# A hybrid scan and attention block on one core: keys handled in three tasks, context decay and rotation tied behind weight chunks, result stores on ScalarE's queue

## The chip, the cores and the metric

The kernel runs on one core of a Trainium2 chip. The metric is device time in microseconds (us), the median of several executions. The engines of the core are named as the profile names them: PE is TensorE (matmuls), DVE is VectorE, ACT is ScalarE, POOL is GpSimd, SP is SyncE. SP, ACT and POOL each have a queue from which they issue DMA transfers, and each engine works through its instructions in the order in which they stand.

## The reference

One transformer block over 256 tokens and 256 context tokens, width 2048. Both are normalised and modulated, then multiplied by one wide matrix `w_in`, whose columns are cut into the inputs of two branches:

```python
xn = rmsnorm(h, norm_gain[l]) * (1.0 + scale) + shift
cn = rmsnorm(hc, norm_gain[l]) * (1.0 + scale_c) + shift_c
aq, ak, av, ag, hq, hff, hfb, hi, hg, ma, mb = split_columns(xn @ w_in[l])
...
q = apply_axial_rope(aq...) * q_scale
k = apply_axial_rope(ak...)
att_branch = window_attention(q, k, v, k_c, v_c, sink_logits[l]) * silu(ag)
```

The other branch, HGRN2, is a two-way gated scan with 16 heads of 128: the forget gates `hff` and `hfb` give a decay per key, the context's own decay gives the state from which the scan starts (forward and backward), and the scan's output is normalised and gated by `silu(hg)`. At the end

```python
y = sigmoid(m_a + b_m[0]) * (hg_branch @ w_o_hgrn) + sigmoid(m_b + b_m[1]) * (att_branch @ w_o_attn)
out = rmsnorm(h + gate * (y @ w_out), final_norm_gain)   # the residual add and the final norm
```

## The kernel before

Everything hangs on weights that stream through once. A weight **chunk** (`wchunk`) is a 512 KB piece of a matrix: SP's queue loads it into a tile `raw` (5 buffers), ACT copies it into `wh` (the leading bits, L78), DVE subtracts to get `wl` (the rest, L79), three buffers each. PE then multiplies: in `proj_tok_g` a chunk is eight matmuls with `wh` (lines L93 and L94 in turn) and four with `wl` (L96). The low ones come last, so `wl` may be late by the time of the eight.

PE runs the instructions in the order in which the code is written (`tc.manual_schedule` names PE alone). On DVE, ACT, POOL and SP a scheduler sets the order by priorities; `wchunk` stands under a high priority, so that the next `wh` and `wl` come first whenever their inputs are due. `tc.issue_after(i)` holds what is written under it back in that order until instruction `i` has been placed: it sets an order and adds no wait of its own.

The program has a start (norms, modulation), a stage that makes forgets, values and keys and stores them in DRAM scratch, eight **pairs** (n = 0 to 7, some 72 us each, 652 to 1270 us in the trace), then attention and the output projections. A pair does the scan of two heads (`pair`), woven with filler (`weave`, `with_gates`, `inputs`) that keeps PE fed: `side_work` is a chain of projection **blocks** (`output_gate`, `merge_out`, `attn_queries`, `attn_gates`), each eight chunks or so. What goes with the blocks and is touched here:

- `output_gate(g)` makes the tiles `sgg`, `attn_queries(j)` the rotated queries `qr`, `attn_gates(j)` the tiles `sga`; each is stored to DRAM scratch (`hg`, `qr`, `ag`) and read back later. `merge_out` stores its tiles `sgm` (`ma`, `mb`) from ACT's queue (L1059).
- `attn_keys(z, t)`: four tasks, one for each half z (0: the 256 tokens, whose keys are rotated; 1: the context's) and row tile t. A task fetches `kr` from scratch `kv`, rotates it into `kx` where z is 0 (`rope`: products with the cosines L1064, with the sines L1069, sum L1072), and is later turned on PE (`turn_tile`, L1092: four transposes into `tkt`), then split by ACT and DVE (L1094, L1095). `inputs` calls `tasks_on` at steps 7, 10, 13 and 16 of the 20 steps of a pair: it finishes the task that was begun at the step before and begins the next.
- `load_forgets(n + 1)`: in the course of pair n it loads the two forget tiles of the next pair (`F0`, `F1`, L1151) and then calls `ctx_decay` for each, which takes a running product over the context half. That is on POOL a memset of `e` (L773 forward, L777 backward), on DVE two scans (L774 or L778) and one combining step (L779).
- `gates` fills in a long product on DVE (L197) whose rows `hgw` are loaded by POOL (L526).

The tiles `sgg`, `sga`, `sgm`, `qr`, `kr`, `kx`, `vr`, `e` and `hsum` all come from one set of **three buffers** (tag "sm"). Whoever takes one waits until the one that held it is done, and if that was a store, until the store has landed.

Of the kernel before, what the change touches and what calls it, by code (L numbers as in the profile page):

```python
# [7 lines left out]
F32 = mybir.dt.float32  # L8
F32R = mybir.dt.float32r
U8 = mybir.dt.uint8  # L10
AF = mybir.ActivationFunctionType
# [27 lines left out]
def block_kernel(ctx: ExitStack, tc: tile.TileContext, x, c, cx, c_ctx, w_ada, b_ada, norm_gain, w_in,  # L39
# [26 lines left out]
            nc.sync.dma_start(rv[:, g], w[row0: row0 + nk * P, co: co + ncol].rearrange("(k p) c -> p k c", p=P))  # L66
        return raw, rv

    last_lo = [None]

    def wchunk(w, row0, nk, col0, ncol):
        cl = col0 if isinstance(col0, tuple) else (col0,)
        raw, rv = wload(w, row0, nk, cl, ncol)
        h = wp.tile([P, 1024], F32R, tag="wh", name="wh", bufs=3)
        lo = wp.tile([P, 1024], F32R, tag="wl", name="wl", bufs=3)
        n = len(cl) * nk * ncol
        with tc.high_priority(PRIO):
            act.activation(h[:, :n], raw[:, :n], AF.Copy)  # L78
            last_lo[0] = dve.tensor_tensor(lo[:, :n], raw[:, :n], h[:, :n].bitcast(F32), op=ALU.subtract).ins  # L79
        parts = [(h[:, g * nk * ncol: (g + 1) * nk * ncol].rearrange("p (k c) -> p k c", k=nk),  # L80
                  lo[:, g * nk * ncol: (g + 1) * nk * ncol].rearrange("p (k c) -> p k c", k=nk)) for g in range(len(cl))]
        return parts if isinstance(col0, tuple) else parts[0]
# [428 lines left out]
    def run(g):  # L511
        for _ in g:
            pass

    def output_gate(g):
        bg = yield from proj_tok_g(w_in, C_HG + 512 * g, x_st, range(2))
        for t in range(2):
            sg = base.tile([P, 512], F32, tag="sm", name="sgg", bufs=3)
            act.activation(sg, bg[t], AF.Sigmoid)
            dve.tensor_tensor(sg, bg[t], sg, op=ALU.mult)  # L520
            nc.gpsimd.dma_start(hg_dr[g][:, t * 512: (t + 1) * 512], sg)

    def gates():

# [21 lines left out]
    with pl("sp", reuse_waits="tile") as sp:  # L546
# [182 lines left out]
        with tc.manual_schedule(engines={mybir.EngineType.PE}):  # L729
            bv0 = proj_tok(w_in, C_HI, x_st, range(4))  # L730
            for g in range(2):
                token_sums(g)
            for t in range(2):
                vo = fp.tile([P, 2, 512], F32, tag="F0", name="vo", bufs=2)
                with tc.high_priority(2 * PRIO):
                    act.activation(vo[:, 0, :], bv0[t], AF.Copy)
                    dve.tensor_copy(vo[:, 1, :], bv0[2 + t])
                nc.gpsimd.dma_start(v_dr[0][t], vo.rearrange("p a c -> p (a c)"))
            run(output_gate(0))
            for g in range(1, 4):  # L740
# [320 lines left out]
    def rope(dst, src, t):  # L1061

        cos = cs[:, K_COS + t * HD: K_COS + (t + 1) * HD].unsqueeze(1).unsqueeze(1).to_broadcast([P, 2, 2, HD])
        dve.tensor_tensor(dst, src.rearrange("p (r h d) -> p r h d", r=2, h=2), cos, op=ALU.mult)  # L1064
# [7 lines left out]
        dve.tensor_tensor(dst, dst, tf, op=ALU.add)  # L1072
# [7 lines left out]
    tasks, task = [], [None]  # L1080

    def tasks_on():


        if task[0]:
            task[0]()
        task[0] = tasks.pop(0)() if tasks else None

    def turn_tile(src, dst, scale=1.0):
        tk = ps.tile([P, 512], F32, tag="tp", name="tkt")  # L1090
        for j in range(4):
            pe.transpose(tk[:, j * P: (j + 1) * P], src[:, j * HD: (j + 1) * HD], ident)  # L1092
        tk = tk.rearrange("p (r c) -> p r c", r=dst[0].shape[1])
        act.activation(dst[0], tk, AF.Copy, scale=scale)  # L1094
        dve.scalar_tensor_tensor(dst[1], tk, scale, dst[0].bitcast(F32), op0=ALU.mult, op1=ALU.subtract)  # L1095

    def attn_keys(z, t):
        def fetch():
            kr = base.tile([P, 512], F32, tag="sm", name="kr", bufs=3)
            nc.gpsimd.dma_start(kr, kv_dr[0][t][:, z * 512: (z + 1) * 512])  # L1100
            if z == 0:
                kx, kr = kr, base.tile([P, 512], F32, tag="sm", name="kx", bufs=3)
                rope(kr.rearrange("p (r h d) -> p r h d", r=2, h=2), kx, t)
            return lambda: turn_tile(kr, [X[:, z: 8: 2, t * P: (t + 1) * P] for X in (XH, XL)])
        return fetch

    def attn_values():
        for t in range(4):
            vr = base.tile([P, 512], F32, tag="sm", name="vr", bufs=3)
            nc.gpsimd.dma_start(vr, kv_dr[1][t % 2][:, (t // 2) * 512: (t // 2 + 1) * 512])  # L1110
            rows = slice(8 + 2 * t, 10 + 2 * t)
            split(XH[:, rows, :], XL[:, rows, :], vr.rearrange("p (r c) -> p r c", r=2))
            yield

    def attn_queries(j):

        def fetch(t):
            qr = base.tile([P, 512], F32, tag="sm", name="qr", bufs=3)
            nc.gpsimd.dma_start(qr, qr_dr[j][:, t * 512: (t + 1) * 512])

            def then():
                q = [XL[:, 8 + 4 * z + 2 * t: 10 + 4 * z + 2 * t, :] for z in range(2)]
                turn_tile(qr, q, HD ** -0.5)
                for z in range(2):
                    nc.gpsimd.dma_start(q_dr[j][z][:, t * 512: (t + 1) * 512].rearrange("p (r c) -> p r c", r=2),
                                        q[z].bitcast(F32))
            return then

        bq = yield from proj_tok_g(w_in, C_Q + 512 * j, x_st, range(2))
        for t in range(2):  # L1130
            qr = base.tile([P, 512], F32, tag="sm", name="qr", bufs=3)
            rope(qr.rearrange("p (r h d) -> p r h d", r=2, h=2), bq[t], t)
            nc.gpsimd.dma_start(qr_dr[j][:, t * 512: (t + 1) * 512], qr)
            tasks.append(lambda t=t: fetch(t))

    def attn_gates(j):
        for hf in range(2):
            bg = yield from proj_col_x_g(w_in, C_G + 512 * j + 256 * hf)
            for i, b in enumerate(bg):
                gs = halves_sum(b, "bb", 2)  # L1140
                sg = base.tile([P, 512], F32, tag="sm", name="sga", bufs=3)[:, :T]
                act.activation(sg, gs, AF.Sigmoid)
                dve.tensor_tensor(sg, sg, gs, op=ALU.mult)
                c0 = (2 * hf + i) * T
                nc.gpsimd.dma_start(ag_dr[j][:, c0: c0 + T], sg)

    def load_forgets(n):
        F = [None, None]
        for d in range(2):
            F[d] = fp.tile([P, 2, 512], F32, tag=f"F{d}", name=f"F{d}", bufs=2 - d)  # L1150
            nc.gpsimd.dma_start(F[d].rearrange("p i t -> p (i t)"), F_dr[d][n])  # L1151
            yield
        for d in range(2):
            ctx_decay(F, (d,))
            yield
        return F

    def side_work():
        values = attn_values()
        tasks.extend(attn_keys(z, t) for z in range(2) for t in range(2))  # L1160
        blocks = (output_gate(1), merge_out(0, 0), output_gate(2), attn_queries(0), merge_out(0, 1), output_gate(3),
                  attn_queries(1), merge_out(0, 2), attn_gates(0), merge_out(0, 3), attn_queries(2), merge_out(1, 0),
                  attn_gates(1), merge_out(1, 1), attn_queries(3), merge_out(1, 2), attn_gates(2), merge_out(1, 3),
                  attn_gates(3))
        for n, g in enumerate(blocks):
            for k, got in enumerate(g):
                yield got
                if n > 16 and k % 2:
                    next(values, None)
            yield 0  # L1170

    side = side_work()
    SIDE = (20, 20, 20, 20, 20, 20, 20, 31)
# [361 lines left out]
```

## Time and profile before

| what | us |
|---|---|
| median of three runs (lowest, highest) | 1605.37 (1603.41, 1609.92) |
| the profiled execution's own time | 1600.81 |
| its span, first to last instruction | 1599.0 |
| PE busy in the span | 1570.7 (98%) |
| DVE busy | 1182.7 (74%) |
| ACT busy | 855.4 (53%) |
| POOL busy | 157.6 (10%) |
| mean granted clock of TensorE | 0.996 |

In the lines of the profile, `wl<-raw,wh` means that the instruction writes tile wl from raw and wh, and L79 is line 79 of the kernel. A timeline row gives the start, the duration, the engine (ACTq is the DMA issuing part of ACT), the instruction, how many are joined in the row (x4), and in square brackets how long the engine stood idle before it and what ended that. A row's duration for matmuls overlaps with the next row's: their pace is the distance of the starts.

### The profile page before, as it was taken

How to read it: one execution, taken by the hardware profiler on the slowest of the kernel's cores; microseconds unless marked ns; L12 is line 12 of the kernel's file. 1: busy time of each engine (PE TensorE's matmuls, PEld its weight loads, DVE VectorE, ACT ScalarE, POOL GpSimd, SP SyncE). 2: the span in 40 equal slices, each digit the busy share in tenths (PEclk: the TensorE clock that was granted, in tenths of full speed). 3: DMA queues.
4: the chain of work that ended last, by engine and by line, in shares of the span. 5: the costliest groups of instructions: out<-in, count | busy, mean ns of one | idle time of the engine just before them, and what ended most of it. 6: DMA issues, size and time to landing. Idle time of an engine off the chain costs nothing.

```text
span 1599.0 us, 27552 instructions
## 1 busy us (share of the span) xinstructions
PE 1570.7 (98%) x10810; PEld 1343.6 (84%) x10810; DVE 1182.7 (74%) x1745; ACT 855.4 (53%) x1338; POOL 157.6 (10%) x312
## 2 busy tenths in 40 slices
PE   7999999999999999999999999999999999999998
PEld 4567899999888888878888888788888888888887
DVE  4449677777888888786978887887977677757764
ACT  4334343333555555656566566565566776744442
POOL 2000000000000000111122222122112100000000
PEclk9999999999999999999999999999999999999999
DMA  9995533434444444776778787676788754558761
GB/s 368 386 386 175 160 120 127 138 130 129 148 134 132 132 132 132 250 235 219 234 251 282 248 266 240 223 263 218 249 275 277 254 160 157 158 172 281 231 209 69
DMA packets 238290, 333.81 MB, mean 209 GB/s; under 512 B 12080, under 2 KB 155856, under 8 KB 237392
## 3 DMA queue, kind: packets, MB, share of 16 engines
q1 hardware_dynamic: 212048, 249.54, 47.8%
q0 software_dynamic: 21216, 70.38, 12.8%
q10 hardware_dynamic: 4896, 12.13, 2.2%
q8 instruction: 85, 1.39, 0.4%
q14 instruction: 45, 0.37, 0.1%
HBM read 300.53 MB, written 31.47 MB: 208 GB/s over the span
## 4 chain that ended last, share of the span: by engine, by line
PE 90%; DMA 4%; DVE 3%; issue 2%; ACT 1%; SPq 0%; POOL 0%; POOLq 0%; DVEq 0%; ACTq 0%
PE pj L93 13%; PE pj L96 13%; PE pj L94 13%; PE pj L147 7%; PE pm L645 4%; PE pj L150 4%; PE pj L645 3%; PE pj L717 2%; PE pj L722 2%; PE pj L719 2%; PE pm L648 2%; PE pm L717 2%; PE pm L722 2%; PE pm L719 2%; PE pj L648 2%
## 5 line engine op out<-in xcount | busy, mean ns | idle before, releaser
L78 ACT ACTIVATE wh<-raw 128x1024 fp32r<-128x1024 f32 x292 | 307.2, 1059 | 262.3 <-PE pj L94 175.2
L79 DVE TENSOR_TENSOR wl<-raw,wh 128x1024 fp32r<-128x1024 f32 x292 | 354.8, 1222 | 125.3 <-ACT wh L78 121.5
L93 PE MATMUL pj<-wh,xHL 128*128 128x512 f32 (+1 forms) x832 | 326.2, 393 | 0.7 <-ACT sg L212 0.7
L94 PE MATMUL pj<-wh,xHL 128*128 128x512 f32 (+1 forms) x832 | 321.4, 388 | 0.0
L96 PE MATMUL pj<-wl,xHL 128*128 128x512 f32 (+1 forms) x832 | 219.7, 388 | 3.6 <-DVE wl L79 3.6
L93 PEld LDWEIGHTS pj<-wh,xHL 128*128 128x128 f32 x832 | 157.4, 189 | 33.1 <-ACT sg L212 1.9
L96 PEld LDWEIGHTS pj<-wl,xHL 128*128 128x128 f32 x832 | 154.6, 189 | 35.5 <-DVE wl L79 4.0
L94 PEld LDWEIGHTS pj<-wh,xHL 128*128 128x128 f32 x832 | 157.6, 189 | 30.2
L620 ACT ACTIVATE wh<-T 128x1024 fp32r<-128x1024 f32 x69 | 73.2, 1061 | 150.9 <-DVE T L601 75.5
L620 ACT ACTIVATE wh<-raw 128x1024 fp32r<-128x1024 f32 x92 | 96.8, 1054 | 62.2 <-PE pj L719 20.2
L147 PE MATMUL pj<-xHL,wh 128*128 128x512 f32 x512 | 129.9, 395 | 0.0
L621 DVE TENSOR_TENSOR wl<-raw,wh 128x1024 fp32r<-128x1024 f32 x92 | 112.1, 1219 | 7.4 <-ACT wh L620 7.3
L147 PEld LDWEIGHTS pj<-xHL,wh 128*128 128x128 f32 x512 | 92.5, 189 | 16.8
L621 DVE TENSOR_TENSOR wl<-T,wh 128x1024 fp32r<-128x1024 f32 x69 | 84.2, 1221 | 28.8 <-ACT wh L620 28.8
L150 PEld LDWEIGHTS pj<-xHL,wl 128*128 128x128 f32 x512 | 69.9, 190 | 5.5 <-issue 0.5
L150 PE MATMUL pj<-xHL,wl 128*128 128x256 f32 x512 | 71.6, 283 | 0.3 <-issue 0.3
L197 DVE SCALAR_TENSOR_TENSOR acc<-hgw,cg,acc 128x512 f32<-128x512 f32 x60 | 44.9, 749 | 29.6 <-DMA hgw<-in_w_ada_dram 29.5
L902 DVE TENSOR_TENSOR A<-A,X 128x512 f32<-128x512 f32 x96 | 61.9, 687 | 1.5 <-ACT Kmt L832 0.7
L526 POOL DMA_DIRECT2D hgw<-in_w_ada_dram x64 | 34.8, 544 | 263.8 <-DVE acc L197 210.0
L645 PE MATMUL pm<-S,wh 128*128 128x512 f32 x224 | 56.7, 395 | 0.8 <-ACT s L652 0.7
L601 DVE TENSOR_TENSOR T<-raw,T 128x1024 f32<-128x1024 f32 x46 | 56.1, 1219 | 0.0
L601 DVE TENSOR_TENSOR raw<-raw 128x1024 f32<-128x1024 f32 x23 | 28.2, 1225 | 35.3 <-DMA raw<-in_w_in_dram 35.3
(359 smaller groups left out, 3037.9 us busy)
## 6 DMA issues: line engine op xcount, KB each, us to landing
raw<-in_w_in_dram SPq DMA_DIRECT2D x300, 512.0 KB, 4.5
raw<-in_w_ada_dram SPq DMA_DIRECT2D x64, 512.0 KB, 8.0
hgw<-in_w_ada_dram POOLq DMA_DIRECT2D x64, 256.0 KB, 4.4
raw<-in_w_o_hgrn_dram SPq DMA_DIRECT2D x32, 512.0 KB, 3.6
raw<-in_w_o_attn_dram SPq DMA_DIRECT2D x32, 512.0 KB, 4.3
raw<-in_w_out_dram SPq DMA_DIRECT2D x28, 512.0 KB, 3.9
F<-F POOLq DMA_DIRECT2D x16, 512.0 KB, 6.6
F<-F ACTq DMA_DIRECT2D x13, 512.0 KB, 4.4
```

What stands on the lines that cost most here:

```text
L78: act.activation(h[:, :n], raw[:, :n], AF.Copy)
L79: last_lo[0] = dve.tensor_tensor(lo[:, :n], raw[:, :n], h[:, :n].bitcast(F32), op=ALU.subtract).ins
L93: pe.matmul(o, s[0], m[0], start=first, stop=False)
L94: pe.matmul(o, s[1], m[0], start=False, stop=False)
L96: pe.matmul(o, s[0], m[1], start=False, stop=last)
L147: pe.matmul(o.rearrange("p (a t) -> p a t", a=2), h[:, j, cs_], xHL[:, :, k0 + j, :T], start=k0 + j == 0, stop=False)
L150: pe.matmul(o[:, :T], lo[:, j, cs_], xH[:, k0 + j, :T], start=False, stop=k0 + j == KT - 1)
L601: dve.tensor_tensor(o, x_, y_, op=ALU.subtract)
L620: act.activation(h, src, AF.Copy)
L621: dve.tensor_tensor(lo, src, h.bitcast(F32), op=ALU.subtract)
L645: pe.matmul(m_[z].rearrange("p (z a t) -> p z a t", z=2, a=2), h[:, k, :], mv(k), start=fresh and k == 0, stop=False, skip_group_check=True)
L648: pe.matmul(pairs_of(m_[z][:, :T]), lo[:, k, :], mv(k)[:, 0], start=False, stop=k == 7, skip_group_check=True)
```

## The change

Four parts. (1) The task of a rotated key is cut in three: fetch at one slot, rotate at the next, turn at the third; the rotation is written under `behind_chunk()`, and it reads `kr` and writes `kx` (before, the loaded tile was named `kx` and the rotated one `kr`). (2) `behind_chunk()` places what stands in it after the latest `wh` on ACT and the latest `wl` on DVE. It is put around the rotation of the keys, around `ctx_decay` (once a chunk has been written), around the split of the attention values, and around the sending of stores. (3) The stores of `sgg`, `qr` and `sga` are no longer issued on POOL's queue where the tile is made; they are put on a list (`outs`) and issued on ACT's queue by `send()` at the next block's first chunk (for `sga` also within the block). A query's fetch task is appended only when its store is sent. (4) Each of the four steps of `attn_values` becomes two, fetch and split, and they are run at each step of the last blocks instead of every second.

```diff
-    last_lo = [None]
+    last_hi, last_lo = [None], [None]
+    def behind_chunk():
+        both = ExitStack()
+        both.enter_context(tc.issue_after(last_hi[0]))
+        both.enter_context(tc.issue_after(last_lo[0]))
+        return both
...
+    outs, tasks, task = [], [], [None]
+    def send():
+        while outs:
+            o = outs.pop(0)
+            nc.scalar.dma_start(*o[:2])
+            tasks.extend(o[2:])
...                                     # output_gate
-            nc.gpsimd.dma_start(hg_dr[g][:, t * 512: (t + 1) * 512], sg)
+            outs.append((hg_dr[g][:, t * 512: (t + 1) * 512], sg))
...
             run(output_gate(0))
+            send()
...                                     # tasks_on
-        if task[0]:
-            task[0]()
-        task[0] = tasks.pop(0)() if tasks else None
+        task[0] = (task[0]() if task[0] else None) or (tasks.pop(0)() if tasks else None)
...                                     # attn_keys: fetch
-            if z == 0:
-                kx, kr = kr, base.tile([P, 512], F32, tag="sm", name="kx", bufs=3)
-                rope(kr.rearrange("p (r h d) -> p r h d", r=2, h=2), kx, t)
-            return lambda: turn_tile(kr, [X[:, z: 8: 2, t * P: (t + 1) * P] for X in (XH, XL)])
+            dst = [X[:, z: 8: 2, t * P: (t + 1) * P] for X in (XH, XL)]
+            if z:
+                return lambda: turn_tile(kr, dst)
+            def rotate():
+                kx = base.tile([P, 512], F32, tag="sm", name="kx", bufs=3)
+                with behind_chunk():
+                    rope(kx.rearrange("p (r h d) -> p r h d", r=2, h=2), kr, t)
+                return lambda: turn_tile(kx, dst)
+            return rotate
...                                     # attn_values
+            yield
             rows = slice(8 + 2 * t, 10 + 2 * t)
-            split(XH[:, rows, :], XL[:, rows, :], vr.rearrange("p (r c) -> p r c", r=2))
+            with behind_chunk():
+                split(XH[:, rows, :], XL[:, rows, :], vr.rearrange("p (r c) -> p r c", r=2))
...                                     # attn_queries
-            nc.gpsimd.dma_start(qr_dr[j][:, t * 512: (t + 1) * 512], qr)
-            tasks.append(lambda t=t: fetch(t))
+            outs.append((qr_dr[j][:, t * 512: (t + 1) * 512], qr, lambda t=t: fetch(t)))
...                                     # attn_gates
-            bg = yield from proj_col_x_g(w_in, C_G + 512 * j + 256 * hf)
+            cols_ = proj_col_x_g(w_in, C_G + 512 * j + 256 * hf)
+            for k in range(4):
+                yield next(cols_)
+                if k == 0 and outs:
+                    with behind_chunk():
+                        send()
+            bg = result(cols_)
...
-                nc.gpsimd.dma_start(ag_dr[j][:, c0: c0 + T], sg)
+                outs.append((ag_dr[j][:, c0: c0 + T], sg))
...                                     # load_forgets
-            ctx_decay(F, (d,))
+            with behind_chunk() if last_lo[0] else ExitStack():
+                ctx_decay(F, (d,))
...                                     # side_work
-                if n > 16 and k % 2:
+                if outs and k == 0:
+                    with behind_chunk():
+                        send()
+                if n > NB - 3:          # NB = 19
                     next(values, None)
             yield 0
+        send()
```

How this moves instructions is seen in the order in which each engine has them. Names carry numbers here: `kx_6698` is one tile. Lines after the change are shifted (`wl` is L86 instead of L79, the matmuls L100, L101 and L103 instead of L93, L94 and L96, the turn L1104 instead of L1092).

**PE in pair 0, where a key is turned.** Before, between the low matmuls of one chunk and the high ones of the next:

```order
L96 MATMUL pj_6575<-wl_6747,xHL_84 128x512
L96 MATMUL pj_6576<-wl_6747,xHL_84 128x512
L1092 MATMUL tkt_6762<-cs_78,kx_6698 128x128 x4
L93 MATMUL pj_6575<-wh_6773,xHL_84 128x512
L94 MATMUL pj_6575<-wh_6773,xHL_84 128x512
```

After, the same place:

```order
L103 MATMUL pj_6567<-wl_6732,xHL_84 128x512
L103 MATMUL pj_6568<-wl_6732,xHL_84 128x512
L1104 MATMUL tkt_6747<-cs_78,kx_6681 128x128 x4
L100 MATMUL pj_6567<-wh_6758,xHL_84 128x512
L101 MATMUL pj_6567<-wh_6758,xHL_84 128x512
```

Before, this is the turn of the second key (t = 1), fetched one slot earlier; after, it is the turn of the first key (t = 0), fetched two slots earlier. The second key's turn now stands in pair 1.

**DVE at the same place** (the rows between two `wl`). Before: `kx_6698` is the second key's loaded and rotated tile, `A` and `X2` belong to the scan of pair 0, `acc` to the long product.

```order
L902 TENSOR_TENSOR A_6346<-A_6346,X2_6347 128x64x8 x2
L79 TENSOR_TENSOR wl_6774<-raw_6771,wh_6773 128x1024
L197 SCALAR_TENSOR_TENSOR acc_6232<-hgw_6234,cg_87,acc_6232 128x512
L1064 TENSOR_TENSOR kx_6698<-kr_6696,cs_78 128x512
L1069 TENSOR_TENSOR rt_6700<-kr_6696,cs_78 128x8x32 x2
L902 TENSOR_TENSOR A_6346<-A_6346,X2_6347 128x32x16 x2
L79 TENSOR_TENSOR wl_6800<-raw_6797,wh_6799 128x1024
L1072 TENSOR_TENSOR kx_6698<-kx_6698,rt_6700 128x512
```

After (`kx_6681` is the first key's rotated tile, `kr_6537` its loaded one; its products with the sines stand three chunks earlier):

```order
L535 TENSOR_TENSOR sgg_6559<-pj_6380,sgg_6559 128x512
L535 TENSOR_TENSOR sgg_6562<-pj_6381,sgg_6562 128x512
L86 TENSOR_TENSOR wl_6732<-raw_6729,wh_6731 128x1024
L918 TENSOR_TENSOR A_6346<-A_6346,X2_6347 128x128x4 x2
L1080 TENSOR_TENSOR kx_6681<-kr_6537,cs_78 128x512
L887 COPY_PREDICATED X2_6347<-mk_79,al_6587 128x4x32
L1088 TENSOR_TENSOR kx_6681<-kx_6681,rt_6683 128x512
L887 COPY_PREDICATED X2_6347<-mk_79,al_6587 128x4x32
L918 TENSOR_TENSOR A_6346<-A_6346,X2_6347 128x64x8 x2
L887 COPY_PREDICATED X2_6347<-mk_79,al_6587 128x4x32
L86 TENSOR_TENSOR wl_6759<-raw_6756,wh_6758 128x1024
```

The rotation that shares a place with this turn now belongs to a key fetched two slots earlier, and its first product with the cosines stands ahead of `wl_6759`; it writes a buffer that `sgg_6559` held.

**POOL's and ACT's queues at the same place.** Before, POOL stores the two `sgg` and fetches the key behind them:

```order
L521 DMA hg1_116<-sgg_6565 128x512
L521 DMA hg1_116<-sgg_6569 128x512
L1151 DMA F1_6722<-F1_1_100 128x1024
L1100 DMA kr_6696<-kv0_1_128 128x512
L1100 DMA kr_6769<-kv0_0_127 128x512
L526 DMA hgw_6234<-in_w_ada_dram 128x512
L773 MEMSET e_6789 128x1 x2
```

After, ACT issues them behind the next chunk's `wh`:

```order
L534 ACTIVATE sgg_6559<-pj_6380 128x512
L534 ACTIVATE sgg_6562<-pj_6381 128x512
L85 ACTIVATE wh_6731<-raw_6729 128x1024
L527 DMA hg1_116<-sgg_6559 128x512
L527 DMA hg1_116<-sgg_6562 128x512
L884 ACTIVATE X2_6347<-al_6587 128x4x32
```

The stores have gone from POOL's queue to ACT's, one chunk later; the second key's fetch is now `kr_6754` on POOL, and its rotation stands two chunks further on.

**DVE in pair 4, the context decay of pair 5.** `e_10017` is the backward scan's tile, `F1_9895` the forget tile that it reads. Before:

```order
L79 TENSOR_TENSOR wl_9920<-raw_9917,wh_9919 128x1024
L197 SCALAR_TENSOR_TENSOR acc_6232<-hgw_6234,cg_87,acc_6232 128x512
L902 TENSOR_TENSOR A_9518<-A_9518,X2_9519 128x128x4 x2
L871 COPY_PREDICATED X2_9519<-mk_79,al_9783 128x4x32 x2
L778 SCALAR_TENSOR_TENSOR e_10017<-F1_9895,zero_6228 128x255
L871 COPY_PREDICATED X2_9519<-mk_79,al_9783 128x4x32
L778 SCALAR_TENSOR_TENSOR e_10017<-F1_9895,zero_6228 128x255
L902 TENSOR_TENSOR A_9518<-A_9518,X2_9519 128x64x8 x2
L779 SCALAR_TENSOR_TENSOR F1_9895<-F1_9895,e_10017 128x2x256
L79 TENSOR_TENSOR wl_9940<-raw_9937,wh_9939 128x1024
```

After:

```order
L86 TENSOR_TENSOR wl_9940<-raw_9937,wh_9939 128x1024
L790 SCALAR_TENSOR_TENSOR e_9955<-F0_9671,zero_6228 128x255 x2
L918 TENSOR_TENSOR A_9518<-A_9518,X2_9519 128x32x16 x2
L795 SCALAR_TENSOR_TENSOR F0_9671<-F0_9671,e_9955 128x2x256
L86 TENSOR_TENSOR wl_9964<-raw_9961,wh_9963 128x1024
L918 TENSOR_TENSOR A_9518<-A_9518,X2_9519 128x16x32 x2
L86 TENSOR_TENSOR wl_9982<-raw_9979,wh_9981 128x1024
L204 SCALAR_TENSOR_TENSOR acc_6232<-hgw_6234,cg_87,acc_6232 128x512
L86 TENSOR_TENSOR wl_10002<-raw_9999,wh_10001 128x1024
L794 SCALAR_TENSOR_TENSOR e_10017<-F1_9895,zero_6228 128x255 x2
```

The scan that reads `F1_9895` stood between `wl_9920` and `wl_9940`; now it stands behind `wl_10002`, four chunks later, and the four `wl` between are ahead of it. POOL's memset of `e_10017` and its load of `F1_9895` stay in the same order to each other.

More of the change, by code (lines that the diff above doesn't have):

```diff
@@ L77, in wchunk @@
         with tc.high_priority(PRIO):
-            act.activation(h[:, :n], raw[:, :n], AF.Copy)
+            last_hi[0] = act.activation(h[:, :n], raw[:, :n], AF.Copy).ins
             last_lo[0] = dve.tensor_tensor(lo[:, :n], raw[:, :n], h[:, :n].bitcast(F32), op=ALU.subtract).ins
@@ L1078, in split @@
         dve.tensor_tensor(dl, src, dh.bitcast(F32), op=ALU.subtract)
-    tasks, task = [], [None]
     def tasks_on():
-        if task[0]:
-            task[0]()
-        task[0] = tasks.pop(0)() if tasks else None
+        task[0] = (task[0]() if task[0] else None) or (tasks.pop(0)() if tasks else None)
     def turn_tile(src, dst, scale=1.0):
@@ L1158, in side_work @@
     def side_work():
-        values = attn_values()
+        values, NB = attn_values(), 19
         tasks.extend(attn_keys(z, t) for z in range(2) for t in range(2))
```

## The prediction

> **What bounds the kernel now.** I read the page's head and chain first, to see which engine sets the time; then what PE waited for in the eight pairs, since the change lies there; then the timelines of the two places that this list names, engine by engine, back to the transfer at their root.
>
> From the page:
>
> ```profile
> span 1599.0 us, 27552 instructions
> PE 1570.7 (98%) x10810; PEld 1343.6 (84%) x10810; DVE 1182.7 (74%) x1745; ACT 855.4 (53%) x1338; POOL 157.6 (10%) x312
> ...
> PE 90%; DMA 4%; DVE 3%; issue 2%; ACT 1%; SPq 0%; POOL 0%; POOLq 0%; DVEq 0%; ACTq 0%
> ```
>
> PE is the bound. The change adds and removes no matmul, so it can win only where PE stands still or runs slowly. PE's waits between 652 and 1270 us (total, times, longest):
>
> ```profile
> PE tkt L1092 <- DVE kx L1072: 3.9, 1, 3.9
> PE pj L96 <- DVE wl L79: 3.6, 1, 3.6
> PE al L977 <- ACT X L868: 0.4, 1, 0.4
> PE pj L150 <- issue: 0.3, 1, 0.3
> ```
>
> Two single waits make 7.5 of the 8.2 us. Both are places that the change touches.
>
> **Stall A, the key's rotation in pair 0.** PE's timeline: the stalled stretch (first three rows), then the same sequence a few us later, undisturbed:
>
> ```profile
> 705.70 1.07 PE L96 MATMUL pj<-wl,xHL 128*128 128x512 f32 x4
> 710.68 1.09 PE L1092 MATMUL tkt<-cs,kx 128*128 128x128 f32 x4 [3.91 <-DVE kx L1072]
> ...
> 716.18 0.39 PE L93 MATMUL pj<-wh,xHL 128*128 128x512 f32 x1
> ...
> 720.72 1.07 PE L96 MATMUL pj<-wl,xHL 128*128 128x512 f32 x4
> 721.63 0.60 PE L1092 MATMUL tkt<-cs,kr 128*128 128x128 f32 x4
> ...
> 723.91 1.07 PE L96 MATMUL pj<-wl,xHL 128*128 128x512 f32 x4
> 724.82 0.39 PE L93 MATMUL pj<-wh,xHL 128*128 128x512 f32 x1
> ```
>
> Low matmuls, a turn, a chunk took 716.18 - 705.70 = 10.48 us; undisturbed they take 724.82 - 720.72 = 4.10. The stall costs 6.38 us, 2.47 more than the 3.91 of waiting. The rest is the clock. Columns here: stretch, its length, busy time of PE, PEld, DVE, ACT, POOL, granted PE clock, DMA share, GB/s:
>
> ```profile
> 711.00:717.00 6.00, 6.00 (x20) 4.87 (x19) 5.47 (x9) 2.33 (x4) 1.20 (x4) 0.62 0.78 262
> 717.00:733.00 16.00, 16.00 (x198) 13.19 (x197) 12.09 (x17) 9.60 (x18) 1.61 (x3) 1.00 0.69 216
> ...
> 1006.00:1010.00 4.00, 4.00 (x12) 3.13 (x12) 4.00 (x6) 2.28 (x5) 0.22 (x1) 0.61 0.78 246
> ```
>
> After either wait the clock is 0.62 or 0.61 for a few us and then 1.00. The Trainium skill, page "TensorE: Matmul & The Clock Gate", section "What's actually happening", says that the array falls to half clock after an idle window of some 3.4 us and comes back after about as long of work; the two rows agree, with waits of 3.91 and 3.61 us. By that rule a wait that merely shrinks to 2 us would cost 2.0 us; in proportion to stall A (6.38 for 3.91) it would cost 3.3, and by the one or the other the time below would be 1595.5 or 1596.8.
>
> What it waited for, on DVE, POOL and ACT:
>
> ```profile
> 698.11 1.28 DVE L902 TENSOR_TENSOR A<-A,X 128x512 f32<-128x512 f32 x2
> 699.31 0.30 DVE L871 COPY_PREDICATED X<-mk,al 128x128 f32<-128x128 uint8 x1
> ...
> 706.23 0.69 DVE L1064 TENSOR_TENSOR kx<-kr,cs 128x512 f32<-128x512 f32 x1 [2.50 <-DMA kr<-kv]
> ...
> 708.71 1.22 DVE L79 TENSOR_TENSOR wl<-raw,wh 128x1024 fp32r<-128x1024 f32 x1
> 709.85 0.69 DVE L1072 TENSOR_TENSOR kx<-kx,rt 128x512 f32<-128x512 f32 x1
> ```
>
> ```profile
> 696.42 1.14 POOL L521 DMA_DIRECT2D hg<-sgg  x2 [2.12 <-DVE sgg L520]
> ...
> 700.18 0.54 POOL L1100 DMA_DIRECT2D kr<-kv  x1 [1.67 <-DMA hg<-sgg]
> ```
>
> ```profile
> 695.87 1.06 ACT L78 ACTIVATE wh<-raw 128x1024 fp32r<-128x1024 f32 x1 [0.64 <-PE pj L94]
> ```
>
> The fetch of the second key waited until a store of `sgg` had landed and freed its buffer (700.18), the data came at 706.23, and the sum was done at 709.85 + 0.69. The turn needed it at 705.70 + 0.91 = 706.61.
>
> **Stall B, the context decay in pair 4.** PE, then DVE, POOL, ACT:
>
> ```profile
> 1001.40 0.39 PE L94 MATMUL pj<-wh,xHL 128*128 128x512 f32 x1
> 1005.40 1.85 PE L96 MATMUL pj<-wl,xHL 128*128 128x512 f32 x4 [3.61 <-DVE wl L79]
> ...
> 1009.84 1.09 PE L96 MATMUL pj<-wl,xHL 128*128 128x512 f32 x4
> ```
>
> ```profile
> 1000.96 0.69 DVE L778 TENSOR_TENSOR_SCAN e<-F,zero 128x255 f32<-128x255 f32 x1 [4.89 <-DMA F<-F]
> ...
> 1004.13 2.36 DVE L79 TENSOR_TENSOR wl<-raw,wh 128x1024 fp32r<-128x1024 f32 x2
> ```
>
> ```profile
> 994.76 0.13 POOL L777 MEMSET e<- 128x1 f32 x2 [5.37 <-issue]
> 995.30 0.53 POOL L1151 DMA_DIRECT2D F<-F  x1 [0.40 <-issue]
> ```
>
> ```profile
> 990.31 0.33 ACTq L1059 DMA_DIRECT2D ma<-sgm  x1
> ```
>
> POOL's memset sat 5.37 us, which the profile does not name; by its order it waits for a buffer that a store of `sgm` (issued near 990) held. The load of `F` behind it was issued at 995.30 and landed at 1000.96; DVE stood 4.89 us with a `wl` behind the scan. An undisturbed chunk, which is also the one with the least slack that I found (PE, then DVE):
>
> ```profile
> 970.64 1.07 PE L96 MATMUL pj<-wl,xHL 128*128 128x512 f32 x4
> ...
> 973.36 1.08 PE L96 MATMUL pj<-wl,xHL 128*128 128x512 f32 x4
> ```
>
> ```profile
> 971.20 2.36 DVE L79 TENSOR_TENSOR wl<-raw,wh 128x1024 fp32r<-128x1024 f32 x2
> ```
>
> A chunk takes 973.36 - 970.64 = 2.72 us; its four low matmuls 0.91 (721.63 - 720.72), a high one (2.72 - 0.91) / 8 = 0.23. From 1001.40 to 1009.84 PE took 8.44 us where 0.23 + 2.72 = 2.95 would do: stall B costs 5.49 us.
>
> **The change, part by part.** *Three tasks for a key.* At A's place on PE now stands the first key's turn, loaded a pair's first slots earlier, so no load is waited for. But its product with the cosines writes the buffer of the first `sgg`, whose store ACT now issues behind a `wh`, at 695.87 + 1.06 = 696.93. With L the time to landing, the product starts at the later of 699.39 (698.11 + 1.28) and 696.93 + L, and the sum is done 0.69 + 0.30 + 0.69 = 1.68 later: at 698.61 + L, needed at 706.61. The `wl` behind it comes 0.30 + 1.28 + 0.30 + 1.22 = 3.10 later still, at 701.71 + L, needed at 706.61 + 2.28 (723.91 - 721.63) = 708.89. So L up to 7.2 us is free. Landings, stores and reads back together (the last line of the answer on tile `hg`, then of that on `qr`, which holds the longest that I found of the three kinds that move; then the issue on ACT, in ns):
>
> ```profile
> DMA to landing us min/median/max: 2.3/3.2/5.0
> ```
>
> ```profile
> DMA to landing us min/median/max: 3.3/5.3/9.5
> ```
>
> ```profile
> L1059 ACTq DMA_DIRECT2D ma<-sgm x8: 326/326/327, 727.1 to 990.3; - x8
> ```
>
> At 5.0 nothing is lost, at 9.5 it is 2.3 us. I take 0, by the row of the same store. The second key waits likewise for its store, but is turned a pair later. Gain at A: 6.38, bounds 4.1 and 6.38. The Trainium skill speaks against this part: "DMA: Bandwidth & Descriptors", section "Anatomy of one DMA — SWDGE (gpsimd) path", says that a completion waits for the receipt of the last byte, with a "surprisingly long delay" for writes to HBM. The trace agrees as far as 9.5 us; by that rule the gain here would be near the lower bound, 4.1, and the median 1595.8, which lies inside the own range of the likeliest case.
>
> *Decay behind a chunk.* The scan that waited moves behind four more `wl`: 4 x 2.72 = 10.9 us, while DVE was 4.89 us early for it. Memset and load stay where they were. The `wl` that was late is now ahead of the scan. Gain at B: 5.49. Bound from below: if the load came 6 us later than at 1000.96 the wait would be back, which nothing in the rows asks for. The scans of the other pairs move in the same way; their load waits are not among PE's four, so 0.
>
> *Stores to ACT.* 32 stores leave POOL: 32 x 0.54 (the issue at 700.18) = 17.3 us of an engine that is 10% busy, worth 0 unless something behind waits. ACT gets 32 x 0.326 = 10.4 us at 53% busy. Cover is the slack between a finished `wl` and its low matmuls. At the tight chunk that is 973.36 - (971.20 + 1.22) = 0.94 us, and two stores of `sga` stand there: 0.65. I take 0; bounds: a loss of 5.49 us if one such place stalls as B did, no gain, since no PE wait outside A and B reaches 0.5 us. What is queued behind a waiting store on ACT is the next `wh`, and PE behind that. Buffers of "sm" stay taken about one chunk, 2.72 us, longer; next to wait would be a memset or fetch on POOL and, behind it, a load of `hgw` for DVE. Queries are fetched a slot later and used only in attention: 0.
>
> *Values in two steps.* The same instructions, the load ahead of the split by one step: 0, with the bounds of the stores.
>
> Sum: -6.38 - 5.49 = -11.87 us on the profiled execution: 1600.81 - 11.87 = 1588.94 (span 1599.0, 1.8 us lie outside it). That execution stands 4.56 below the median of 1605.37; in proportion the median becomes 1605.37 x 1588.94 / 1600.81 = 1593.5, 0.74% less. A difference under 0.5%, 8.0 us, can hardly be told from none.
>
> **The rivals.** *One stall stays, or one new one comes.* A stays if the store that frees the buffer of `kx` lands later than 7.2 us, B if the load of `F` is late by 6 more. For it: 9.5 us is in the rows. Time: 1593.5 plus 5.49 or 6.38, some 1599.5.
>
> *The change does not reach the stalls* (the buffers are as short as before and both waits move on to a later chunk, or two new ones come): 1605. For it: three buffers remain, and all stores now hold theirs longer. Against: every `wl` between is now ahead of the waiting instruction.
>
> *Slower: ACT held by its own stores.* ACT works in order; a store whose tile DVE has not finished holds the next `wh`. Each hold that outlasts the slack far enough for a 3.6 us wait costs 5.49. With A and B gone it takes four such holds, in some fourteen sendings, to be 0.5% slower: -11.87 + 4 x 5.49 = +10.1, about 1615.5. Against: tile and store are a chunk apart, 2.72 us, and the first store of `sgg` would find its tile done.
>
> **How the numbers follow.** Both stalls go: 0.58, 1593.5, with its own range of 1588 to 1598 (the three runs spread over 6.5 us). One stays or comes: 0.22. No net change: 0.11. Slower: 0.09. The range from 1588 to 1604 leaves out most of the last two and a little below. Faster by over 0.5% means below 1597.3: the first case almost whole and a fifth of the second, 0.60; same 0.31; slower 0.09.
>
> **What would show it.** After: no PE wait on `kx` (then L1088) or on `wl` (L86) above 1 us in the pairs, a granted clock of 1.00 in pairs 0 and 4, the first product of `kx` waiting at most some 3 us for DMA `hg`, and no row on ACT in which a store waits for DVE for more than a us. Wrong would be: a wait of 3.5 us or more in any pair, with a clock near 0.6 behind it, most likely at a `wl` behind a rotation or behind a store on ACT.

## The result, and the profile after

The change takes 1594.01 us, the median of six runs (1591.82 to 1594.79), against 1604.39 of before, measured beside it (six runs, 1600.47 to 1610.22): a ratio of 0.9929, 95% interval 0.9912 to 0.9946. On a second occasion it was 0.9931 (0.9915 to 0.9947). That is faster by 0.7%, as forecast (1593.5, 0.74% less). The profiled execution of after took 1593.52 us.

The page of after, span and busy times:

```profile
span 1591.7 us, 27553 instructions
PE 1567.9 (99%) x10810; PEld 1341.4 (84%) x10810; DVE 1182.9 (74%) x1745; ACT 855.4 (54%) x1338; POOL 140.5 (9%) x280
```

PE, DVE and ACT run as many instructions as before (PE's busy time falls by 2.8 us, as it works less at half clock); POOL is 17.1 us lighter, the 32 stores. What PE waited for between 652 and 1270 us (total, times, longest):

```profile
PE tkt L1104 <- DMA qr<-qr: 2.5, 1, 2.5
PE pj L157 <- issue: 0.6, 1, 0.6
PE pj L154 <- DVE sgm L1073: 0.5, 1, 0.5
PE ob L1012 <- DVE X L998: 0.3, 1, 0.3
```

The waits on `kx` and on `wl` are gone, and a new one stands at the head. First the place of stall A, on DVE and then on PE:

```profile
700.92 0.69 DVE L1080 TENSOR_TENSOR kx<-kr,cs 128x512 f32<-128x512 f32 x1 [1.61 <-DMA hg<-sgg]
...
701.73 0.69 DVE L1088 TENSOR_TENSOR kx<-kx,rt 128x512 f32<-128x512 f32 x1
...
703.93 1.22 DVE L86 TENSOR_TENSOR wl<-raw,wh 128x1024 fp32r<-128x1024 f32 x1
```

```profile
705.25 1.07 PE L103 MATMUL pj<-wl,xHL 128*128 128x512 f32 x4
706.16 0.60 PE L1104 MATMUL tkt<-cs,kx 128*128 128x128 f32 x4
```

The rotation waits 1.61 us for the store whose buffer it takes, as the prediction had it, but it ends at 702.42, 3.7 us before the turn at 706.16, which starts with no bracket: no idle time.

The place of stall B, on POOL, DVE and PE:

```profile
988.72 0.13 POOL L793 MEMSET e<- 128x1 f32 x2 [4.61 <-DMA ma<-sgm]
989.25 0.54 POOL L1176 DMA_DIRECT2D F<-F  x1 [0.41 <-PE pj L103]
```

```profile
1000.61 1.22 DVE L86 TENSOR_TENSOR wl<-raw,wh 128x1024 fp32r<-128x1024 f32 x1
1001.74 1.26 DVE L794 TENSOR_TENSOR_SCAN e<-F,zero 128x255 f32<-128x255 f32 x2
```

```profile
998.97 1.07 PE L103 MATMUL pj<-wl,xHL 128*128 128x512 f32 x4
1001.69 1.07 PE L103 MATMUL pj<-wl,xHL 128*128 128x512 f32 x4
```

The memset still waits 4.61 us (5.37 before), now with its cause named: the store of `sgm`. The load goes out at 989.25, and the scan comes 12.5 us later, at 1001.74, with no wait; PE goes from chunk to chunk in 2.72 us. The clock in these two stretches, and in the one of the new wait (columns as before; the granted clock is the number behind POOL's):

```profile
700.00:712.00 12.00, 12.00 (x56) 9.91 (x55) 11.08 (x19) 7.89 (x13) 1.34 (x6) 1.00 0.61 197
992.00:1004.00 12.00, 12.00 (x55) 9.93 (x54) 12.00 (x17) 8.47 (x14) 0.54 (x1) 1.00 0.63 200
...
1207.00:1211.00 4.00, 4.00 (x15) 3.25 (x14) 1.98 (x3) 2.34 (x6) 1.99 (x3) 0.67 0.70 239
```

**The new wait, C, in pair 7.** PE, POOL, ACT's queue:

```profile
1206.43 1.09 PE L1104 MATMUL tkt<-cs,qr 128*128 128x128 f32 x4 [2.46 <-DMA qr<-qr]
...
1207.74 0.63 PE L101 MATMUL pj<-wh,xHL 128*128 128x512 f32 x1
1208.17 0.63 PE L100 MATMUL pj<-wh,xHL 128*128 128x512 f32 x1
```

```profile
1200.93 0.54 POOL L1139 DMA_DIRECT2D qr<-qr  x1 [2.63 <-DMA ag<-sga]
```

```profile
1195.70 0.97 ACTq L527 DMA_DIRECT2D ag<-sga  x2
```

POOL's fetch of the last queries waits 2.63 us until a store of `sga`, now issued by ACT at 1195.70, has landed and given up its buffer. The data comes at 1206.3, but PE reaches the turn of this tile, one slot behind the fetch, at 1203.97: it idles for 2.46 us, then steps 0.43 us a matmul instead of 0.23. Before, the same fetch and its turn stood 13.4 us apart, and the fetch was ahead of the stores of `sga`:

```profile
1195.69 0.54 POOL L1119 DMA_DIRECT2D qr<-qr  x1 [6.34 <-ACT bH L1019]
...
1207.21 1.12 POOL L1145 DMA_DIRECT2D ag<-sga  x2 [4.86 <-DVE sga L1143]
```

```profile
1209.10 0.66 PE L1092 MATMUL tkt<-cs,qr 128*128 128x128 f32 x4
```

**Where the time went, by pair.** A pair's length here is the time from its first `tw` matmul on PE to that of the next pair (the last one to the first matmul of attention), worked out from the starts in each trace. The column of the values is the stretch ahead of pair 0, from the first `pm` matmul to the first `tw`; the last column is the time of that profiled execution:

| kernel | values | pair 0 | 1 | 2 | 3 | 4 | 5 | 6 | 7 | us |
|---|---|---|---|---|---|---|---|---|---|---|
| before | 458.3 | 77.6 | 71.4 | 71.8 | 72.2 | 73.2 | 72.9 | 70.6 | 79.3 | 1600.81 |
| before, again | 460.3 | 77.8 | 71.1 | 71.8 | 72.2 | 74.2 | 72.3 | 72.9 | 79.1 | 1604.88 |
| after | 458.4 | 71.3 | 72.5 | 71.8 | 72.2 | 68.6 | 72.2 | 70.4 | 83.2 | 1593.52 |
| after, again | 460.6 | 71.4 | 71.8 | 71.8 | 72.2 | 69.1 | 72.2 | 70.4 | 81.2 | 1594.35 |
| decay alone | 460.0 | 77.0 | 70.9 | 71.8 | 72.2 | 68.9 | 72.3 | 70.9 | 79.7 | 1597.06 |
| keys alone | 460.3 | 72.5 | 73.2 | 71.8 | 72.2 | 73.6 | 73.6 | 70.4 | 79.2 | 1599.5 |
| stores alone | 460.3 | 77.7 | 72.0 | 71.8 | 72.2 | 72.2 | 72.3 | 72.7 | 85.1 | 1608.9 |
| keys and decay | 459.9 | 71.3 | 72.7 | 71.8 | 72.2 | 68.3 | 73.0 | 70.4 | 80.4 | 1593.57 |

Pairs 2 and 3, which no stall touches, agree in all rows to 0.1 us. From before to after (differences taken before rounding): pairs 0 and 1 together -5.3 us (they belong together, since two turns moved from 0 to 1), pairs 4 and 5 -5.3, pair 7 +3.9. Between the two repeats: -5.7, -5.2, pair 6 -2.5, pair 7 +2.1.

### The profile page after: what moved, and what is told of

The parts are those of the page before. It is cut to its first block, busy times and chain, and to the rows that moved or that the text cites. A ratio compares the mean times of both kernels' runs of the same rounds, so it can differ in the third digit from the quotient of the medians.

```text
span 1591.7 us, 27553 instructions
## 1 busy us (share of the span) xinstructions
PE 1567.9 (99%) x10810; PEld 1341.4 (84%) x10810; DVE 1182.9 (74%) x1745; ACT 855.4 (54%) x1338; POOL 140.5 (9%) x280
## 5 line engine op out<-in xcount | busy, mean ns | idle before, releaser
L86 DVE TENSOR_TENSOR wl<-raw,wh 128x1024 fp32r<-128x1024 f32 x292 | 354.4, 1219 | 122.1 <-ACT wh L85 116.2
L100 PE MATMUL pj<-wh,xHL 128*128 128x512 f32 (+1 forms) x832 | 325.0, 392 | 0.7 <-ACT sg L219 0.7
L101 PE MATMUL pj<-wh,xHL 128*128 128x512 f32 (+1 forms) x832 | 320.3, 386 | 0.0
L103 PE MATMUL pj<-wl,xHL 128*128 128x512 f32 (+1 forms) x832 | 218.5, 386 | 0.0
L100 PEld LDWEIGHTS pj<-wh,xHL 128*128 128x128 f32 x832 | 156.9, 189 | 32.7 <-ACT sg L219 1.9
L101 PEld LDWEIGHTS pj<-wh,xHL 128*128 128x128 f32 x832 | 156.9, 189 | 29.9
L103 PEld LDWEIGHTS pj<-wl,xHL 128*128 128x128 f32 x832 | 154.0, 188 | 31.4
L635 ACT ACTIVATE wh<-T 128x1024 fp32r<-128x1024 f32 x69 | 73.2, 1061 | 149.6 <-DVE T L616 74.0
L154 PE MATMUL pj<-xHL,wh 128*128 128x512 f32 x512 | 130.3, 395 | 0.6 <-DVE sgm L1073 0.5
L154 PEld LDWEIGHTS pj<-xHL,wh 128*128 128x128 f32 x512 | 92.4, 189 | 18.0 <-DVE sgm L1073 0.9
```

Source lines behind the costliest of these rows:

```text
L100: pe.matmul(o, s[0], m[0], start=first, stop=False)
L101: pe.matmul(o, s[1], m[0], start=False, stop=False)
L103: pe.matmul(o, s[0], m[1], start=False, stop=last)
L154: pe.matmul(o.rearrange("p (a t) -> p a t", a=2), h[:, j, cs_], xHL[:, :, k0 + j, :T], start=k0 + j == 0, stop=False)
L635: act.activation(h, src, AF.Copy)
```

## The experiments

**The kernel before, once more.** No edit.

> The kernel before once more, for a second profile: its runs lie between 1600.5 and 1610.2 us, and its profiled execution, 1600.8, is near the lowest of them, while the profile after is only 7.3 us shorter, against 10.4 between the medians. Theory one (stalls A and B and nothing else): PE's two waits on kx and on wl are there again, 3.5 to 4 us each, and no third over 1 us, whatever the time. Theory two (the runs of before differ by further stalls that come and go): an execution of 1603 or more shows a third wait of PE of 2 us or more in the pairs, or a longer A or B; one near 1601 shows the same two.

It took 1604.88 us. PE's waits in the pairs:

```profile
PE pj L96 <- DVE wl L79: 4.6, 1, 4.6
PE tkt L1092 <- DVE kx L1072: 3.8, 1, 3.8
PE pj L93 <- issue: 2.1, 1, 2.1
```

Theory two: both stalls are there, B a us longer, and a third wait of 2.1 us in pair 6, in which PE waits for nothing that the profile names; pair 6 is 2.3 us longer in the table, and the stage of the values 2.0. So the profile on which the prediction worked was a short one: it was some 4 us shorter than most executions. That third wait came at the same place in two of the later profiles too (stores alone, keys as before), in neither of the whole change; what points to its cause stands in the last section.

**The decay alone.**

```diff
-            ctx_decay(F, (d,))
+            with behind_chunk() if last_lo[0] else ExitStack():
+                ctx_decay(F, (d,))
```

> The kernel before with one part of the change alone: the context decay is tied behind a chunk. Theory one (each part takes away its own stall): PE's wait on wl in pair 4 is gone and its half clock with it, the wait of 3.9 us on kx stays; 5.5 us less than before, a ratio of 0.9966. Theory two (the buffers are as short as before, the wait moves to a later wl): the ratio is 0.999 to 1.001, with a new PE wait of 3 us or more in one of the pairs.

1597.99 us, six runs against twenty of before (1606.3): 0.9947 (0.9928 to 0.9967). The wait on `wl` is gone, the one on `kx` stays:

```profile
PE tkt L1099 <- DVE kx L1079: 3.9, 1, 3.9
PE pj L154 <- DVE rt L1076: 0.8, 1, 0.8
```

Theory one; pair 4 falls to 68.9 us and pair 0 stays at 77.0. The gain of 0.53% is above the 0.34% expected, though its interval takes that in.

**The keys alone.** Before, with `attn_keys` and `tasks_on` of after:

```diff
+            def rotate():
+                kx = base.tile([P, 512], F32, tag="sm", name="kx", bufs=3)
+                with behind_chunk():
+                    rope(kx.rearrange("p (r h d) -> p r h d", r=2, h=2), kr, t)
+                return lambda: turn_tile(kx, dst)
+            return rotate
```

> The kernel before with the keys alone in three tasks, their rotation behind a chunk; stores stay on POOL, the decay where it was. Theory one: PE's wait on kx is gone, the one on wl in pair 4 stays; 6.4 us less, a ratio of 0.9960. Theory two (the wait moves on, the buffers being as short): 0.999 to 1.001, with a new PE wait of 3 us or more in pair 0 or 1.

1600.91 us: 0.9966 (0.9952 to 0.9980), nine runs. Pairs 0 and 1 together fall from 149.0 to 145.7, and the wait on `wl` in pair 4 stays (4.0 us; the other 0.7 is in pair 0):

```profile
PE pj L103 <- DVE wl L86: 4.7, 2, 4.0
PE al L984 <- ACT X L875: 3.0, 3, 1.1
```

Theory one, with a smaller gain than the 6.4 us: 0.34% is 5.4. In this profile it is smaller still, 3.3 us in pairs 0 and 1, where PE now waits 0.7 us on `wl` and 0.8 and 1.1 at `al`. This part does two things at once, an earlier fetch and a rotation behind a chunk; no run takes them apart.

**The stores alone.** Before, with `outs` and `send` of after, the stores on `nc.scalar`.

> The kernel before with the stores alone moved to ACT's queue and sent a chunk later; keys, decay and values as before. Theory one (A and B are made by where the rotation and the decay stand): both stay, A up to 1 us longer since its store goes out later; a ratio of 1.000 to 1.003, above that if the later store of sga makes a third wait as in the profile after (4 us more, 1.003 to 1.005). Theory two (POOL's queue is what holds the loads): both waits shrink under 2 us and the ratio is 0.994 or less.

1606.26 us: 1.0001 (0.9988 to 1.0014), twelve runs. Both stalls stay (B is shorter here, 2.8 us), and C is there without any other part of the change:

```profile
PE tkt L1106 <- DVE kx L1088: 4.0, 1, 4.0
PE pj L103 <- DVE wl L86: 2.8, 1, 2.8
PE tkt L1106 <- DMA qr<-qr: 2.6, 1, 2.6
PE pj L100 <- issue: 2.0, 1, 2.0
```

Theory one. That it was no slower in the median although pair 7 is 5.8 us longer in this profile suggests that C is not as long in most executions; a gain elsewhere would look the same.

**The change with a free buffer for the last queries.**

```diff
-            qr = base.tile([P, 512], F32, tag="sm", name="qr", bufs=3)
+            if j == 3 and t == 1:
+                qr = fp.tile([P, 2, 512], F32, tag="F0", name="F0", bufs=2)[:, 0, :]
+            else:
+                qr = base.tile([P, 512], F32, tag="sm", name="qr", bufs=3)
```

> The changed kernel with one more edit: the second row tile of the last queries is fetched into a tile of F0 that is free in pair 7, so that it waits for none of the three shared buffers. Theory one (in the profile after, PE's wait of 2.5 us on qr with its half clock, 4.2 us, came from a fetch held by a store of sga): that wait is gone, and the time is 4 us below the change's 1594.0, a ratio to before of 0.990 (0.988 to 0.992). Theory two (that wait is a single execution's, or the fetch is as late from another cause): the ratio is the change's, 0.993 (0.991 to 0.995).

1593.55 us: 0.9917 (0.9899 to 0.9934), against 1606.35 of before, as in the next three. The wait on `qr` is gone and no wait in the pairs reaches 1 us, but the median hardly moved: the 4 us did not come. The ratio lies in the ranges of both theories; this version was run again, below.

**The change without the tied decay.**

> The changed kernel without the tie of the context decay behind a chunk; all else as changed. Theory one (the place of the scan alone makes stall B): PE waits 3 us or more on wl in pair 4 again, 5.5 to 8.5 us more than the change, a ratio to before of 0.997 to 0.999. Theory two (moving the stores off POOL's queue had freed the load in time): no such wait, the ratio is the change's 0.993.

1603.6 us: 0.9985 (0.9971 to 1.0000), twelve runs spread from 1599.7 to 1609.4. B is back in pair 4, 3.0 us long. The row below counts two more waits on `wl`, 1.8 us in pair 1 and 0.3 in pair 0; there DVE waited for no transfer, but was at work on rotations, scans and other products ahead of the `wl`. In pair 7 there is a wait of 2.4 at the turn of `qr`:

```profile
PE pj L103 <- DVE wl L86: 5.1, 3, 3.0
PE tkt L1104 <- DVE hsum L165: 2.4, 1, 2.4
```

Theory one: the stores off POOL's queue do not free the load in time. Without the tie the change is worth 0.15%, with it 0.71%, a difference of some 9 us.

**The change with the keys as before.**

> The changed kernel with the keys as they were: fetch and rotation in one task, the rotation not tied. Theory one: PE waits 3.5 us or more on kx in pair 0 again, 5.4 to 6.4 us more than the change, a ratio to before of 0.9965 to 0.998. Theory two (the later stores and the tied decay free the buffer in time): no wait above 2 us there, ratio 0.993.

1602.37 us: 0.9975 (0.9963 to 0.9987). A is back, 4.1 us, and so is the unnamed wait of pair 6:

```profile
PE tkt L1106 <- DVE kx L1088: 4.1, 1, 4.1
PE pj L100 <- issue: 2.2, 1, 2.2
```

Theory one, with more than the 5.4 to 6.4 us named: by the ratios (0.9975 against 0.9929) the change gives up 7.4 us without this part. A part of that may be the unnamed wait, which the theory did not have: in this profile pair 6 is 74.4 us long, against 70.4 after.

**The change with the stores on POOL.**

```diff
-            outs.append((hg_dr[g][:, t * 512: (t + 1) * 512], sg))
+            nc.gpsimd.dma_start(hg_dr[g][:, t * 512: (t + 1) * 512], sg)
...                                     # likewise for qr and ag
```

> The changed kernel with the stores back on POOL's queue, at the place where each tile is made; keys, decay and values as changed. Theory one (the stores bring nothing, and sent later they hold the buffers that make the wait on qr): neither the waits on kx and wl nor the one on qr; 4 us below the change, a ratio to before of 0.990 (0.988 to 0.992). Theory two (the stores are needed: on POOL they stand ahead of loads): a PE wait of 2 us or more in a pair, ratio 0.993 or more.

1594.0 us: 0.9927 (0.9907 to 0.9948). Neither stall A nor B nor C; the longest wait is an unnamed one of 2.05 us, here in pair 1, which the profile puts down to no store. So the new queue is not needed for the gain, against theory two, but leaving it out did not bring the 4 us of theory one either.

**Four versions on one chip.** To see whether C costs 4 us in every execution, the change, the free buffer, the stores on POOL, and, new, the keys and the decay alone (before with the first two edits above, nothing else) ran together.

> The changed kernel as it is, beside the next three on one chip. All four profiles so far with the stores on ACT and the shared buffers lost 2.7 to 5.8 us in pair 7, where the two versions that cannot have the wait on qr, or have the stores on POOL, lost 1.2 and -0.2; yet the medians of those two, 1593.6 and 1594.0, hardly differ from the change's 1594.0. Theory one (the wait on qr is in every execution): this profile shows it again, 2 to 3 us and half clock, and the ratio to before is 0.0025 above that of the version with the keys and the decay alone. Theory two (it comes and goes, or is paid elsewhere by the others): the ratios of all four lie within 0.0015.

> The version that fetches the last queries into a free tile of F0, again, on one chip with the change. Theory one: 4 us less than the change. Theory two: within 0.0015 of it; its profile then shows what stands in the place of the 4 us.

> The version with the stores back on POOL, again, on one chip with the change. Theory one: 4 us less than the change, no wait on qr in pair 7. Theory two: within 0.0015 of the change.

> The kernel before with the keys in three tasks and the decay tied behind a chunk, nothing else of the change: stores on POOL, values as before. If these two parts make the whole gain, as 0.9947 and 0.9966 for each alone say, the ratio to before is the change's 0.993 or lower (0.989 to 0.994), and PE waits neither on kx nor on wl for over 1 us. If stores or values bring something of their own, it is 0.995 or more.

| version | us | ratio to before (1606.13) | 95% interval |
|---|---|---|---|
| the change | 1595.35 | 0.9931 | 0.9915 to 0.9947 |
| free buffer | 1594.26 | 0.9924 | 0.9907 to 0.9941 |
| stores on POOL | 1593.25 | 0.9916 | 0.9897 to 0.9934 |
| keys and decay alone | 1593.38 | 0.9914 | 0.9896 to 0.9932 |

The profile of the change, once more:

```profile
PE tkt L1104 <- DMA qr<-qr: 0.8, 1, 0.8
PE al L993 <- ACT Kmt L981: 0.8, 1, 0.8
```

C is 0.8 us here instead of 2.5, with no half clock behind it, and pair 7 is 81.2 us long instead of 83.2. The fetch waited just as long for its buffer:

```profile
1203.48 0.54 POOL L1139 DMA_DIRECT2D qr<-qr  x1 [2.43 <-DMA ag<-sga]
```

What differs is its landing: the turn starts at 1207.55, 4.1 us after the issue, where it was 1206.43 - 1200.93 = 5.5. So C grows and shrinks with the landing, as theory two has it; all intervals overlap, and the four ratios lie within 0.0017, just above the 0.0015 named. Keys and decay alone give the whole gain: 0.0086, and the two apart 0.0053 + 0.0034 = 0.0087. The version with these two alone is no worse than the change; whether it, or the one with the stores on POOL, is better by the 2 us of the medians the intervals do not tell.

## Why the prediction was right

*Stall A.* The mechanism was right, and the size nearly so: 5.3 and 5.7 us (pairs 0 and 1 in the two pairs of profiles) and 5.4 (keys alone, timed) against 6.38. The new wait on the store's landing was 1.61 us and stayed on DVE. What was missing is small waits that the sum set to 0: after, PE waits 0.5 us at L154 for `sgm` on DVE, a product that now stands behind the scan, the rotation and two `wl`; in other profiles with the keys in three tasks up to 0.85.

*Stall B.* Right, mechanism and size: 5.3 and 5.2 us in pairs 4 and 5 against 5.49. The timed runs say more, 0.0053 for the decay alone, 8.5 us with an interval from 5.3 to 11.6, and B does vary: 3.61 us of waiting in one profile of before, 4.61 in the other, where the memset stood 6.53 us instead of 5.37. In both it starts 0.1 us after a store of `sgm` has landed (at 994.67 and 998.93), so the inference from the order was right.

*The stores: 0.* Right for the total, by 1.0001 for the stores alone. The step that was too kind is "buffers of sm stay taken about one chunk longer": the prediction named a fetch on POOL as the next to wait and gave it no time, but in pair 7 it is 0.6 to 2.6 us of waiting on DMA `qr` in the profiles with the stores on ACT and the shared buffers (without the tied decay it was 2.4 on DVE at the same turn), and at 2.4 and above half clock on top. The sentence behind it, "Queries are fetched a slot later and used only in attention: 0", was wrong: PE turns the fetched tile one slot later, still in the pair. Before, the last fetch landed at 1198.95 for a turn at 1209.10; after, at 1206.29 for a turn that PE reached at 1203.97. This was the rival "one new one comes" (1599.5, 0.22). It came in the profile, and the time still was that of the likeliest case.

*The values: 0.* The version with neither the stores nor the values changed, keys and decay alone, shows no difference that the intervals tell; the values by themselves were not run.

*From the profile to the median.* This is the step that held by two errors that cancel, so that 1593.5 came within a us of 1594.0 is in part luck. Within the first two profiles the change is worth 7.3 us, not 11.87: 10.6 in pairs 0, 1, 4 and 5, less 3.9 in pair 7, and some tenths elsewhere. Scaling 1600.81 to the median of before took for granted that a longer execution is longer everywhere. It is not: the repeat of before was 4.1 us longer through a wait of 2.1 us in pair 6, 2.0 us in the values stage and a us in B. After, a longer execution has the 2.0 us of the values too, but not the wait in pair 6 in any of the profiles of the whole change or of its two useful parts. From repeat to repeat, 1604.88 to 1594.35, it is 10.53 us, as between the medians. That the pair 6 wait went is part of the gain that was not foreseen; no run was made to show why, but the last section has what the traces say.

*The slower rival*, ACT held by its own stores, did not come: no PE wait of after in the pairs is on `wh` or `wl`. The sum let the stores of `sgg` go out when the `wh` ahead of them had ended; they are issued from 696.07 on, while that `wh` is still running, from 695.79 to 696.85:

```profile
695.79 1.06 ACT L85 ACTIVATE wh<-raw 128x1024 fp32r<-128x1024 f32 x1 [0.64 <-PE pj L101]
696.07 0.93 ACTq L527 DMA_DIRECT2D hg<-sgg  x2
```

## What to carry to other kernels

In an engine that works in order, what costs is not the late transfer but the urgent instruction that stands behind it: look for the one wait on a DMA that has a needed producer behind it, and move it past as many of those as the transfer is late. A store that is sent later holds its buffer later, so follow who takes that buffer next before you delay one. And take a second profile of the kernel before a sum against its median: one execution here was 4 us shorter than most others, and a stall's size varied by a us with the landing of one store.

## What the runs showed of the hardware

**The clock.** A wait of PE need not be as long as the 3.6 us of stall B to bring half clock. After C's 2.46 us the granted clock was 0.67 from 1207 to 1211; without the tied decay 2.42 us of idling was followed by steps of 0.43 us. The unnamed waits of pair 6 fall on both sides: behind 2.10 us (before, again) the clock was 1.00, behind 2.16 us (keys as before) it was 0.57. With the stores alone a wait of 2.63 us was followed by some matmuls at the usual pace, 0.22 to 0.28 us apart, and only 1.4 us after its end by steps of 0.43:

```profile
1220.12 0.63 PE L1106 MATMUL tkt<-cs,qr 128*128 128x128 f32 x4 [2.63 <-DMA qr<-qr]
...
1221.04 0.39 PE L100 MATMUL pj<-wh,xHL 128*128 128x512 f32 x1
1221.27 0.48 PE L101 MATMUL pj<-wh,xHL 128*128 128x512 f32 x1
1221.55 0.63 PE L100 MATMUL pj<-wh,xHL 128*128 128x512 f32 x1
1221.98 0.63 PE L101 MATMUL pj<-wh,xHL 128*128 128x512 f32 x1
```

The Trainium skill, page "TensorE: Matmul & The Clock Gate", section "What's actually happening", gives one idle window of some 3.4 us as the condition and says that the window runs freely. The late drop would fit such a window, but the waits of 2.16 to 2.63 us are shorter than the condition, and here the measurement decides.

**The waits without a name.** The traces also hold the DMA queues that the page of the profile marks "instruction". One of them, q8, moves 85 packets of 16 KB; PE has 10810 matmuls and 10810 weight loads, 254 to a packet, so these are likely its own instructions. In all eight waits of PE in the pairs that have no named cause (0.3 to 2.2 us, in seven of the profiles), PE goes on 1.3 to 1.6 us after such a packet has been moved. The four over 2 us:

| profile | packet, us | PE goes on | after the packet |
|---|---|---|---|
| before, again, pair 6 | 1163.40 to 1164.66 | 1166.05 | 1.4 |
| stores alone, pair 6 | 1161.98 to 1162.91 | 1164.28 | 1.4 |
| keys as before, pair 6 | 1157.98 to 1158.91 | 1160.40 | 1.5 |
| stores on POOL, pair 1 | 801.19 to 802.12 | 803.49 | 1.4 |

In pair 6 PE waits behind a run of 128 small matmuls and four transposes. In the five profiles with the keys as before, the packet starts at most 0.5 us ahead of that run, and with the wait 1.5 to 1.8 us into it; in the nine with the keys in three tasks it starts 2.3 us or more ahead, and there is no wait. This points to late loading of instructions and to the keys as what moved it; it is not shown, since no run moves the packets alone, and with the decay alone PE went on 0.8 us after the packet, with a wait of only 0.2 us.
